# Even layer: the gating branch moved in front of the attention, and the queries and keys of heads 2 and 3 made inside it

## The chip, the cores and the metric

The kernel runs on one core of one Trainium2 chip (a trn2 part). The metric is the device time of one run in microseconds (us), the median of several runs. One further run was taken with the hardware profiler; all rows of the trace come from that run. The engines are PE (matrix products), DVE and POOL (elementwise work, reductions), ACT (activation functions and copies) and SP (which here issues transfers); they run side by side and wait for each other by semaphores.

## The reference, cut to what matters

The program is a two-layer block over 512 tokens and 256 context tokens, in float32, with a model width of 1024. The change lies in the mixer of layer 0, the even layer:

```python
u, v, q, k, vv = jnp.split(h @ w_in, [A_WIDTH, 2 * A_WIDTH, KV_START, KV_START + B_QK_WIDTH], axis=-1)
q = apply_rope(q.reshape(b, s_len, 2 * B_HEADS, HEAD_DIM), cos, sin)
k = apply_rope(k.reshape(b, s_len, 2 * B_HEADS, HEAD_DIM), cos, sin)
...
o = lax.map(lambda qb: diff_attn(qb, k_all, v_all, lam), q_blocks)
y = jnp.concatenate([chunk_mlp(u, v, w_s, b_s), diff_out(o, subln_g, lam_init)], axis=-1) @ w_out
```

There are two branches. The gating branch (`chunk_mlp`) takes `u` and `v`, four groups of 128 columns each: both go through an exact gelu, `v` is normalised over the 128 columns of a group, mixed along each chunk of 128 tokens by a matrix `w_s` of the group, and multiplied with `u`. The attention branch has four heads; each computes two softmaxes and subtracts `lam` times the second from the first (`diff_attn`). The context tokens go through the same steps with keys of the context alone. Both branches are laid side by side and projected with `w_out`.

## The kernel before, in words

Everything is kept with features on the partitions and tokens along the free axis: 512 token columns (TX) and 256 context columns (TC), 768 (TA) together. A float32 operand is split into a high and a low part of reduced precision, and each product is made of three matrix products (`mm3`, its lines L115, L116 and L117): high by high, high by low, low by high. The split of a weight block is a cast on ACT (L89) and a subtraction on POOL (L92); its load (L86) is issued on SP's queue. The buffers of loaded and split weights form a ring, so a load waits until an older buffer has been used.

The even layer runs in these stages, in the order in which PE meets them.

1. Queries and keys, in two halves. Half 0 makes those of heads 0 and 1, half 1 those of heads 2 and 3; each is 8 steps over the input features with 4 blocks of 128 columns, first for the tokens (512 wide) and then for the context (256 wide). Half 0 also normalises the inputs. Between the steps stand slabs of the modulation's weights (`ada_ahead` loads one, `ada_some` multiplies it, L370): work of another part of the layer that is laid here. The finished queries and keys go through `rope` (two DVE and two POOL operations each: shuffle L263, cosine L264, sine L265, sum L266).
2. The values V, 8 steps with 6 blocks of tokens, with one slab per step.
3. The attention, by head and, within a head, by pair of query blocks `qp`: 0 and 1 are tokens (scores against 768 keys), 2 is context (256 keys). One `softmax_diff` makes the scores (L553 and L554), their maximum (DVE, L555), the exponential (ACT, L557) and the difference (DVE, L563); `attend` then transposes it (PE, L575), splits it (ACT L131, DVE L132) and multiplies it with V. `stack` splits the queries and keys of the next head (ACT L272, L287, L288, DVE L276, L290). `norm` normalises a finished head.
4. Filling products. PE would stand still in the attention while a softmax runs. So `gated(i)`, one block of 128 columns of `u` (i = 0 to 3) or `v` (i = 4 to 7), 24 products of 512 and 24 of 256 columns, is given to the scheduler at a lower priority than the heads (`high_priority` lifts the heads above work written before them): it is taken where nothing of the heads is ready. In the kernel before, blocks 4 to 7 fill heads 0 and 1, and blocks 0 to 3 heads 2 and 3.
5. After head 1, the four gelus of `v` stand together on ACT (L643), and the exponentials of head 2 are held behind them (`issue_after(last.ins)`), so that ACT changes between the tables of gelu and exponential only there. Then `turn(g)` transposes a group of `v` on PE (L655), takes it back (ACT L656) and makes its statistics on DVE (L659 and L660); `mix(g)` normalises it (ACT L670, DVE L672), multiplies it with the mixing matrix (PE L673) and adds the bias (DVE L674). The mixes stand last, behind head 3.
6. `slab` loads the weights of the projection (`even_out`, 512 KB each), `cat` multiplies `u` and `v` (L717) and splits the eight inputs, and the projection (384 wide) follows.

The scheduler works out the order of each engine's instructions ahead of the run from priorities and from which operands are ready; on the chip every engine then goes through its own list strictly in order. SP's queue is such a list too.

## Time and profile before

| | |
|---|---|
| time, median of 3 runs | 1572.99 us (1571.8 to 1576.91) |
| time of the profiled run | 1574.88 us |
| its span in the trace | 1573.0 us |
| mean granted PE clock | 0.994 of full speed |
| busy: PE, DVE, ACT, POOL | 1514.1, 1073.0, 727.8, 826.1 us |

Of the span, the part that the change touches begins at 39.6 us (half 0 of the queries and keys) and ends at 333.7 us (first product of the projection). A row of the windows view gives a stretch of time, its length, the busy time of PE, of PE's weight loads, of DVE, ACT and POOL with their instruction counts, the granted PE clock (1.00 is full speed), the share of the transfer engines that was busy, and GB/s. A row of the timeline gives start, length, engine, line, operation and operands, and in brackets how long the engine had stood idle and what it waited for. A row of one line of code gives the shortest, the median and the longest duration in ns and the first and last start. Busy PE is not PE at full speed: where the clock is halved, each product simply takes longer.

### The profile page before, as it was taken

Reading aid. Unit: us, or ns where it says so; the run is one execution under the profiler, and the core shown is the slowest. Engines: PE = TensorE matmul, PEld = TensorE weight load, DVE = VectorE, ACT = ScalarE, POOL = GpSimd, SP = SyncE. Lnnn points to the kernel's source line nnn. Section 1 sums busy time; section 2 is a strip of 40 time slices with the busy share of each in tenths; the row PEclk is TensorE's granted clock in tenths of the full one; section 3 lists DMA queues with packets and bytes.
Section 4 is the critical chain, followed back from the end, with each engine's and each line's share of the span. In section 5 each row is a group of like instructions: output and inputs, shape, how many; then the busy total and the mean of one; then the engine's idle time right before and its main releaser. Section 6 shows DMA issues by size and latency. Waiting matters only on the chain.

```text
span 1573.0 us, 24994 instructions
## 1 busy us (share of the span) xinstructions
PE 1514.1 (96%) x9563; PEld 1352.0 (86%) x9563; DVE 1073.0 (68%) x1938; ACT 727.8 (46%) x1490; POOL 826.1 (53%) x558
## 2 busy tenths in 40 slices
PE   6999987999999999999999999999999999999998
PEld 4776876889999999999999988777869889999997
DVE  3720788765697787888786486765667966666665
ACT  2422677553553333333333354555645644444444
POOL 0464211050347777777776544531314399898982
PEclk9999999999999999999999999999999999999999
DMA  9835100033223333344542212200224133333301
GB/s 331 311 131 201 45 8 1 1 134 134 68 74 121 114 95 128 128 150 165 167 157 85 79 47 61 68 28 15 68 95 173 54 104 103 104 100 108 95 21 54
DMA packets 53416, 162.26 MB, mean 103 GB/s; under 512 B 6193, under 2 KB 8625, under 8 KB 45617
## 3 DMA queue, kind: packets, MB, share of 16 engines
q1 hardware_dynamic: 46240, 135.37, 25.7%
q10 hardware_dynamic: 7056, 25.30, 5.0%
q8 instruction: 75, 1.23, 0.3%
q14 instruction: 45, 0.36, 0.1%
HBM read 158.55 MB, written 2.10 MB: 102 GB/s over the span
## 4 chain that ended last, share of the span: by engine, by line
PE 85%; DVE 10%; ACT 3%; issue 1%; DMA 0%; DVEq 0%; SPq 0%; ACTq 0%
PE pw L115 12%; PE pw L116 12%; PE pw L117 11%; PE pb L116 8%; PE pb L117 8%; PE pb L115 8%; PE pf L115 4%; PE pf L116 4%; PE pf L117 4%; PE pb L1635 2%; PE pb L1624 2%; PE pf L370 2%; PE pw L1586 1%; PE pw L1594 1%; DVE t L49 1%
## 5 line engine op out<-in xcount | busy, mean ns | idle before, releaser
L116 PE MATMUL pw<-ax,w 128*128 128x384 f32 (+2 forms) x740 | 237.0, 321 | 3.5 <-DVE ax L49 2.2
L115 PE MATMUL pw<-ax,w 128*128 128x384 f32 (+2 forms) x740 | 235.9, 321 | 3.6 <-DVE q L49 1.9
L117 PE MATMUL pw<-ax,w 128*128 128x384 f32 (+2 forms) x740 | 236.4, 320 | 0.1
L785 DVE SCALAR_TENSOR_TENSOR xT<-pb,mod,xT 128x512 f32<-128x512 f32 (+3 forms) x204 | 143.2, 708 | 129.3 <-PE pb L117 128.8
L92 POOL TENSOR_TENSOR w<-raw,w 128x512 fp32r<-128x512 f32 (+1 forms) x76 | 115.4, 1526 | 219.0 <-ACT w L89 196.3
L49 POOL TENSOR_TENSOR w<-raw,w 128x512 fp32r<-128x512 f32 x122 | 185.0, 1531 | 48.8 <-ACT w L49 48.7
L49 POOL TENSOR_TENSOR w<-t,w 128x512 fp32r<-128x512 f32 x99 | 148.7, 1505 | 55.7 <-ACT w L49 55.7
L115 PE MATMUL pb<-hh,w 128*128 128x512 f32 x480 | 171.4, 357 | 1.2 <-DVE xT L785 1.2
L117 PE MATMUL pb<-hh,w 128*128 128x512 f32 x480 | 171.7, 358 | 0.4 <-DVE w L49 0.4
L116 PE MATMUL pb<-hh,w 128*128 128x512 f32 x480 | 171.3, 357 | 0.0
L115 PE MATMUL pw<-T,w 128*128 128x384 f32 (+1 forms) x508 | 156.6, 310 | 2.5 <-DVE hs L991 1.2
L116 PE MATMUL pw<-T,w 128*128 128x384 f32 (+1 forms) x508 | 157.0, 310 | 1.2 <-DVE T L132 1.2
L117 PE MATMUL pw<-T,w 128*128 128x384 f32 (+1 forms) x508 | 157.0, 310 | 0.0
L116 PEld LDWEIGHTS pw<-ax,w 128*128 128x128 f32 x740 | 140.8, 190 | 10.4 <-DVE ax L477 3.1
L115 PEld LDWEIGHTS pw<-ax,w 128*128 128x128 f32 x740 | 140.0, 190 | 10.6 <-DVE q L49 2.7
L115 PE MATMUL pf<-ax,w 128*128 128x256 f32 (+2 forms) x428 | 140.7, 329 | 3.9 <-ACT f L596 2.8
L117 PEld LDWEIGHTS pw<-ax,w 128*128 128x128 f32 x740 | 140.7, 190 | 3.3 <-DVE w L954 0.4
L116 PE MATMUL pf<-ax,w 128*128 128x256 f32 (+2 forms) x428 | 139.6, 326 | 0.0
L117 PE MATMUL pf<-ax,w 128*128 128x256 f32 (+2 forms) x428 | 139.5, 326 | 0.0
L49 POOL TENSOR_TENSOR hh<-hs,hh 128x768 fp32r<-128x768 f32 (+1 forms) x42 | 77.3, 1842 | 94.7 <-ACT hh L49 70.7
L49 POOL TENSOR_TENSOR w<-rawo,w 128x512 fp32r<-128x512 f32 x59 | 103.8, 1759 | 28.6 <-ACT w L49 28.6
L240 DVE SCALAR_TENSOR_TENSOR junk<-ar,cb 128x1024 bf16<-128x1024 f32 x64 | 105.7, 1651 | 0.0
(412 smaller groups left out, 3909.2 us busy)
## 6 DMA issues: line engine op xcount, KB each, us to landing
raw<-ffn_in SPq DMA_DIRECT2D x44, 1024.0 KB, 5.1
ar<-ada SPq DMA_DIRECT2D x24, 1024.0 KB, 6.8
ar<-ada ACTq DMA_DIRECT2D x48, 512.0 KB, 3.6
rawo<-ffn_out SPq DMA_DIRECT2D x88, 256.0 KB, 3.0
raw<-odd_out SPq DMA_DIRECT2D x28, 256.0 KB, 2.7
raw<-qk SPq DMA_DIRECT2D x16, 256.0 KB, 7.9
raw<-uv SPq DMA_DIRECT2D x16, 256.0 KB, 2.7
raw<-even_out SPq DMA_DIRECT2D x8, 512.0 KB, 3.9
```

The source lines that it names most:

```text
L49: self.tail[key] = fn(*args, **kw)
L92: eng.tensor_tensor(lo, raw, hi.bitcast(F32), ALU.subtract)
L115: mm(out, s[0], m[0], start=start, stop=False, **kw)
L116: mm(out, s[0], m[1], start=False, stop=False, **kw)
L117: return mm(out, s[1], m[0], start=False, stop=stop, **kw)
L240: return self.nc.vector.scalar_tensor_tensor(junk, t, 1.0, self.cb[who], ALU.mult, ALU.mult, accum_out=self.acc[who][:, col:col + 1])
L370: nc.tensor.matmul(ps[32 * q:32 * q + 32, :w], cst[:, k, :], t[:, w * q:w * q + w], start=k == 0, stop=k == KT - 1, skip_group_check=True)
L785: ins = self.nc.vector.scalar_tensor_tensor(h, ps[:, r], self.modcol(l, j, m, who), h, ALU.mult, ALU.add)
L1586: nc.tensor.matmul(ps[:, st:en], Q, K[g][p][:, b0 * P:b1 * P], start=p == 0, stop=p == 1, skip_group_check=True)
L1594: last = nc.tensor.matmul(ps[:, en:en + TC], Q, K[g][p][:, TX:], start=p == 0 and not edge, stop=p == 1, skip_group_check=True)
L1624: last = nc.tensor.transpose(pt[:, x * P:(x + 1) * P], es[2 * (x % 2) + x // 2][:, kb * P:(kb + 1) * P], self.ident)
L1635: nc.tensor.matmul(po[64 * h:64 * h + 64, :], V[vb][:, 64 * g:64 * g + 64], t[:, h * TC:h * TC + TC], start=kb == 0, stop=kb == nb - 1, sk ...
```

## The change

In the front part only heads 0 and 1 get their queries and keys. Half 1 is cut out, and with it the place of six slabs, which now stand in the V stage, two at every second step. The weights of heads 2 and 3 are laid out anew on the host (`qk1`) as four blocks of 128 columns, like those of `gated`.

Behind V comes the gating branch of `v`: `gated(4)` to `gated(7)` one after the other, each followed by its gelu, with `turn` one block behind; then `lam`, the reciprocal roots of the statistics and the four `mix`. Their PSUM banks come from `bank` in place of `fill`. Then come the heads. They are filled by `block(0)` to `block(3)` (queries and keys of heads 2 and 3, with their rope) in heads 0 and 1, and by `gated(0)` to `gated(3)` in heads 2 and 3. The gelus of `u` and the product with `v` stay where they were, behind the last exponential. Buffers move with it: the rope tables stay to the end of the attention, its shuffle buffer has one copy in place of two, the pool `f3` has four slots in place of eight and the four `v` have a tag of their own.

```diff
+        self.ropep = tc.alloc_tile_pool(name="rope0", bufs=1, side="left", reuse_waits="tile")
+        self.sh_bufs = 1
+        self.ropep.tile([P, 512], F32, name=self.uid("sh"), tag="sh", bufs=1)
+        tabs = [self.ropep.tile([P, TX], F32, name=n, tag=n, bufs=1) for n in ("cos", "sin")]
...
-        def f3(tag="f3", bufs=8):
+        def f3(tag="f3", bufs=4):
             return R1.tile([P, TA], F32, name=self.uid(tag), tag=tag, bufs=bufs)
...
-        tabs = []
...
-        for half, heads in enumerate(((0, 1), (2, 3))):
-            w2 = [self.wide(), self.wide()]
-            accx = [w[:, h * 512:(h + 1) * 512] for w in w2 for h in range(2)]
-            W = []
...
-                elif k % 2:
-                    ada_ahead(1)
-                    ada_some()
...
+        w2 = [self.wide(), self.wide()]
+        accx = [w[:, h * 512:(h + 1) * 512] for w in w2 for h in range(2)]
+        keys = (0, 1, 4, 5)
+        W = []
+        for k in range(KT):
+            t = self.adap.tile([P, 2, 512], F32R, name=self.uid("wq"), tag="wq", bufs=2) if k in (2, 5) else None
+            with tc.issue_after(self.last_slab.ins):
+                W.append(self.blocks(a["qk"][k], 512, t=t))
+                if k > 3:
+                    with tc.issue_after(self.last_w.ins):
+                        ada_ahead(1)
+                if k == 7:
+                    for t, n in zip(tabs, ("cos", "sin")):
+                        nc.sync.dma_start(t, a[n])
...
+            if k % 2:
+                ada_some()
+                ada_ahead(1)
+        for n in range(4):
+            evacuate(accc[n], keys[n], slice(TX, TA))
+        for n in (0, 4, 1, 5):
+            self.rope(qk[n][:, :TX], qk[n][:, :TX], tabs)
...
                 self.mm3(acc[tb], [t[:, c] for t in AX_[k]], W, k == 0, k == KT - 1)
-            ada_ahead(1)
-            ada_some()
+            for _ in range(1 + k % 2):
+                ada_some()
+                ada_ahead(1)
         for ps in acc:
             h = Rv.tile([P, 512], F32R, name=f"vhi{len(vhi)}")
             l = Rv.tile([P, 512], F32R, name=f"vlo{len(vhi)}")
@@ -525,13 +521,12 @@
             ada_ahead(1)
             ada_some()
         with tc.issue_after(self.last_w.ins):
-            sguT = self.load(Rv, a["sguT"], [P, 512], "sguT")
+            sgu = self.sumsq()
+            sguT = sgu[:, :512]
+            nc.sync.dma_start(sguT, a["sguT"])
             sgub = self.load(Rv, a["sgub"].partition_broadcast(P), [P, 512], "sgub")
-        here = tc.cur_priority
-        self.ropep.release()
         self.adap.release()
 
-        self.lam()
         self.subg = self.load(self.p0, a["subln"], [P, 1], "subg")
...
         def gated(i, after=None):
 
             W = self.blocks(a["uv"][i])
-            u = f3()
+            u = f3() if i < 4 else f3("rv")
             for off, T, A in ((0, TX, axx), (TX, TC, axc)):
-                ps = self.fill()[:, :T]
+                ps = (self.fill if off or i < 4 else self.bank)()[:, :T]
                 self.dense(ps, W, A, after, 0 if off else 2)
                 nc.scalar.copy(u[:, off:off + T], ps)
             raw[i] = u
...
-        def gelu(i, after):
-            with tc.issue_after(after.ins):
+        def gelu(i, after=None):
+            with tc.issue_after(after.ins) if after else ExitStack():
                 return nc.scalar.activation(raw[i], raw[i], AF.Gelu)
 
         halves = ((0, 4), (4, 2))
-        stats = Rv.tile([P, 24, 6], F32, name="stats")
+        stats = sgu[:, 512:656].rearrange("p (t v) -> p t v", v=6)
...
-        with tc.high_priority(offset=tc.cur_priority - here):
-            QK = {0: stack(0)}
-        for t in range(2):
-            head(t)
+        def block(n):
+
+            key = (2, 6, 3, 7)[n]
+            W = self.blocks(a["qk1"][n])
+            qk[key] = f3()
+            for c, A in ((slice(0, TX), axx), (slice(TX, TA), axc)):
+                ps = self.fill()[:, :c.stop - c.start]
+                self.dense(ps, W, A)
+                evacuate(ps, key, c)
+            self.rope(qk[key][:, :TX], qk[key][:, :TX], tabs)
+
+        QK = {0: stack(0)}
+        for g in range(4):
+            gated(4 + g)
+            last = gelu(4 + g)
+            if g:
+                turn(g - 1)
+        turn(3)
+        with tc.issue_after(last.ins):
+            self.lam()
+        rs = self.rstd_small(mv[:, :, 1], 24, 1.0, "sf")
+        nb = self.small(24, "sf", 3)
+        nc.vector.scalar_tensor_tensor(nb, mv[:, :, 0], -1.0, rs, ALU.mult, ALU.mult)
+        for g in range(4):
+            mix(g, rs)
         here = tc.cur_priority
-        for i in (4, 5, 6, 7):
-            gated(i)
-        for i in (4, 5, 6, 7):
-            last = gelu(i, self.last_exp)
-        with tc.high_priority(offset=tc.cur_priority - here), tc.issue_after(last.ins):
-            head(2)
-            head(3)
-        after = self.last_sum
-        for g in range(4):
-            turn(g)
-            gated(g, after if g == 3 else None)
+        for t, jobs in enumerate(((block, 0, 1), (block, 2, 3), (gated, 0, 1), (gated, 2))):
+            for i in jobs[1:]:
+                jobs[0](i, *([self.last_exp] if t == 3 else []))
+            with tc.high_priority(offset=tc.cur_priority - here), tc.issue_after(last.ins):
+                head(t)
+        gated(3, self.last_sum)
         Ra.release()
+        self.ropep.release()
+        self.sh_bufs = 2
         self.close_ring()
         self.ada_open(2)
         self.open_ring(1024, 3, 8)
...
         slab(0)
         slab(1)
-        rs = self.rstd_small(mv[:, :, 1], 24, 1.0, "sf")
-        nb = self.small(24, "sf", 3)
-        nc.vector.scalar_tensor_tensor(nb, mv[:, :, 0], -1.0, rs, ALU.mult, ALU.mult)
-        for g in range(4):
-            mix(g, rs)
         cat = {}
         for k in order:
             if k < 4:
...
+    qk = ew[:, 1024:2048].reshape(D, 2, 2, 2 * P)
+    r["qk"] = c(qk[:, :, 0].reshape(KT, P, 512))
     r["v0"] = c(ew[:, 2048:2560])
...
+    r["qk1"] = cols(c(qk[:, :, 1].reshape(D, 2, 2, P).transpose(0, 2, 1, 3).reshape(D, 512)))
     r["uv"] = cols(ew[:, 0:1024])
```

The scheduler's order shows what comes of it. The rows below are PE's around the first scores of head 0; `ax` with `w` is a filling product or one of `gated`, `kh`, `kl` with `qa`, `qb` are scores, `ident` is a transposition. In the kernel before, the first scores stand behind the 512 wide half of the first `gated` alone:

```order
L116 MATMUL pf_1914<-ax_326,w_1910 128x512
L117 MATMUL pf_1914<-ax_325,w_1910 128x512
L553 MATMUL pw_1344<-kh_1328,qa_1322 128x512
L554 MATMUL pw_1344<-kh_1328,qa_1322 128x256
L553 MATMUL pw_1344<-kl_1329,qa_1322 128x512
...
L554 MATMUL pw_1352<-kl_1335,qb_1323 128x256
L115 MATMUL pf_1940<-ax_311,w_1905 128x256
L116 MATMUL pf_1940<-ax_312,w_1905 128x256
```

In the changed kernel they stand behind all four `gated` of `v` and the transpositions of its group 2 (`rv_1221`), and the block that follows them is one of queries and keys:

```order
L116 MATMUL pf_1334<-ax_329,w_1304 128x256
L117 MATMUL pf_1334<-ax_328,w_1304 128x256
L650 MATMUL pb_1361<-ident_103,rv_1221 128x128 x4
L650 MATMUL pb_1375<-ident_103,rv_1221 128x128 x2
L548 MATMUL pw_1635<-kh_1049,qa_1043 128x512
L549 MATMUL pw_1635<-kh_1049,qa_1043 128x256
...
L549 MATMUL pw_1643<-kl_1056,qb_1044 128x256
L115 MATMUL pf_1506<-ax_314,w_1497 128x512
...
L116 MATMUL pf_1506<-ax_325,w_1502 128x512
L650 MATMUL pb_1383<-ident_103,rv_1307 128x128 x4
L117 MATMUL pf_1506<-ax_324,w_1502 128x512
```

What moved is three and a half blocks of `gated` and three of the four turns to a place ahead of the scores; the last turn and the mixes lie within head 0.

The next rows are ACT's between the last exponentials of head 3 (`e`) and the first cast of the projection's weights (`w_3133<-raw_3134` before, `w_3217<-raw_3218` in the changed kernel). Before, the normalisation of the mixes (L670, twelve in all) and the copies of the turns stand there:

```order
L557 ACTIVATE e_2715,sa_2704<-pw_2711,sa_2703 128x256
L643 ACT_TABLE_LOAD
L643 ACTIVATE f_555_2810<-f_555_2810 128x768
L643 ACTIVATE f_564_2895<-f_564_2895 128x768
L131 CAST ath_2637<-pb_2632 128x512
...
L656 COPY f_375_2102<-pf_3047 128x256
L587 COPY o_2459<-pb_2722 128x256
L612 ACTIVATE sq_2739<-o_2459 128x768
L670 ACTIVATE f_354_1913<-f_354_1913,sf_3156,sf_3144 128x128 x3
L670 ACTIVATE f_361_1976<-f_361_1976,sf_3156,sf_3144 128x128 x3
...
L643 ACTIVATE f_582_3065<-f_582_3065 128x768
L89 CAST w_3133<-raw_3134 128x1024
```

In the changed kernel they are gone, and all three gelus of `u` stand ahead of the last splits of the difference (`ath`), since the blocks of `u` are done earlier:

```order
L552 ACTIVATE e_3075,sa_3064<-pw_3071,sa_3063 128x256
L638 ACT_TABLE_LOAD
L638 ACTIVATE f_405_2340<-f_405_2340 128x768
L638 ACTIVATE f_412_2403<-f_412_2403 128x768
L638 ACTIVATE f_503_2766<-f_503_2766 128x768
L131 CAST ath_3012<-pb_3007 128x512
L131 CAST ath_3027<-pb_3022 128x512
...
L131 CAST ath_3088<-pb_3083 128x512
L582 COPY o_2819<-pb_3082 128x256
...
L131 CAST ax_3240<-f_405_2340 128x768
L638 ACTIVATE f_597_3148<-f_597_3148 128x768
L131 CAST ax_3246<-f_412_2403 128x768
L89 CAST w_3217<-raw_3218 128x1024
```

The third place is PE's list behind the last scores of head 3 (`pw` with `kh` and `kl`, 256 wide). Before, filling products (`pf_2981`) stand right behind them, and the transpositions of the difference come between these:

```order
L165 MATMUL pb_2561<-ones,sq_2457 128x128 x2
L554 MATMUL pw_2711<-kh_2390,qb_2379 128x256
L554 MATMUL pw_2711<-kl_2391,qb_2379 128x256
L115 MATMUL pf_2981<-ax_311,w_2972 128x512
L116 MATMUL pf_2981<-ax_312,w_2972 128x512
...
L117 MATMUL pf_2981<-ax_317,w_2972 128x512
L575 MATMUL pb_2632<-ident_100,e_2593 128x128
L115 MATMUL pf_2981<-ax_319,w_2977 128x512
...
L117 MATMUL pf_2981<-ax_325,w_2977 128x512
L115 MATMUL pb_2631<-ath_2637,vhi_1274 128x256
```

In the changed kernel the scores are followed by transpositions and products with V (`ath`, `vhi`) alone, and the filling products `pf_3149` come again behind the head's last sum of squares (L165), since `gated(3, self.last_sum)` holds all but their first six back:

```order
L549 MATMUL pw_3071<-kh_2687,qb_2676 128x256
L549 MATMUL pw_3071<-kl_2688,qb_2676 128x256
L115 MATMUL pb_2991<-ath_2997,vhi_1007 128x256
L570 MATMUL pb_3007<-ident_103,e_2953 128x128
...
L117 MATMUL pb_2991<-ath_3027,vlo_1028 128x256
L195 MATMUL pb_3038<-q_2937,ones 128x512
L195 MATMUL pb_3041<-q_2942,ones 128x256
L570 MATMUL pb_3083<-ident_103,e_3050 128x128
...
L117 MATMUL pb_3082<-ath_3088,vlo_1028 128x256
L165 MATMUL pb_3102<-ones,sq_3099 128x128 x4
L165 MATMUL pb_3108<-ones,sq_3099 128x128 x2
L115 MATMUL pf_3149<-ax_318,w_3140 128x512
```

What moved is the filling: of 72 and 72 filling products (512 and 256 wide) behind the first scores of head 3, the changed kernel has 24 and 48 left.

More of the change, by code (lines that the diff above doesn't have):

```diff
@@ L447, in ctx_load, with evacuate @@
                 hc.extend(t[:, n, :] for n in range(4))
-        tabs = []
-        def evacuate(ps, n, c, heads):
-            h = heads[n % 2]
-            key = h if n < 2 else 4 + h
-            if key not in qk:
-                qk[key] = f3()
-            nc.scalar.mul(qk[key][:, c], ps, 0.125 if n < 2 else 1.0)
+        for key in (0, 4, 1, 5):
+            qk[key] = f3()
+        def evacuate(ps, key, c):
+            nc.scalar.mul(qk[key][:, c], ps, 0.125 if key < 4 else 1.0)
         with tc.issue_after(self.last_slab.ins):
@@ new lines, in even @@
+        for n in range(4):
+            evacuate(accx[n], keys[n], slice(0, TX))
+        bk = [self.bank() for _ in range(2)]
+        accc = [b[:, h * TC:(h + 1) * TC] for b in bk for h in range(2)]
+        for k in range(KT):
+            for n in range(4):
+                self.mm3(accc[n], W[k][n], axc[k], k == 0 and n % 2 == 0, k == KT - 1)
+            if k % 2:
+                ada_some()
+                ada_ahead(1)
+        for n in range(4):
+            evacuate(accc[n], keys[n], slice(TX, TA))
@@ L652, in turn @@
             for off, n in halves:
-                ps = self.fill()
+                ps = self.bank()
                 for i in range(n):
@@ L665, in mix @@
             for off, n in halves:
-                pw = self.fill()
+                pw = self.bank()
                 for i in range(n):
```

50 lines of the change are left out of this document (12 added, 38 removed).

## The prediction

> **What bounds the kernel now.** I read the page first, for the engines' shares and for the chain that ends last:
>
> ```profile
> PE 1514.1 (96%) x9563; PEld 1352.0 (86%) x9563; DVE 1073.0 (68%) x1938; ACT 727.8 (46%) x1490; POOL 826.1 (53%) x558
> PE 85%; DVE 10%; ACT 3%; issue 1%; DMA 0%; DVEq 0%; SPq 0%; ACTq 0%
> ```
>
> PE bounds the whole, so a moved product wins nothing by itself; only PE's waits can be won or lost. The windows view, cut at the stages and at the heads' first scores, shows where these lie (columns: stretch, length, then busy PE, weight loads, DVE, ACT, POOL; clock; share of the transfer engines; GB/s):
>
> ```profile
> 39.60:81.80 42.20, 40.50 (x231) 30.99 (x232) 28.98 (x51) 20.29 (x39) 21.18 (x15) 1.00 0.79 290
> 81.80:121.80 40.00, 40.00 (x242) 30.54 (x243) 10.04 (x20) 7.82 (x16) 26.85 (x20) 1.00 0.45 156
> 121.80:163.40 41.60, 41.60 (x206) 28.13 (x206) 7.21 (x10) 13.35 (x21) 14.52 (x12) 1.00 0.46 167
> 163.40:169.00 5.60, 5.59 (x25) 4.30 (x23) 5.56 (x10) 3.81 (x8) 1.80 (x2) 1.00 0.23 67
> 169.00:200.60 31.60, 29.61 (x184) 26.09 (x184) 21.83 (x40) 18.86 (x40) 6.66 (x4) 1.00 0.12 39
> 200.60:214.60 14.00, 12.66 (x77) 11.28 (x78) 12.73 (x23) 9.44 (x20) 3.37 (x2) 1.00 0.07 20
> 214.60:250.30 35.70, 27.61 (x160) 22.96 (x158) 28.43 (x70) 26.36 (x50) 4.37 (x3) 0.86 0.00 0
> 250.30:271.60 21.30, 19.44 (x130) 17.48 (x130) 17.09 (x44) 15.46 (x34) 3.40 (x3) 1.00 0.00 1
> 271.60:294.70 23.10, 21.97 (x140) 19.55 (x141) 20.43 (x53) 12.84 (x29) 1.20 (x1) 1.00 0.00 1
> 294.70:333.70 39.00, 35.06 (x220) 29.20 (x219) 27.70 (x115) 24.72 (x50) 5.83 (x3) 1.00 0.19 68
> 333.70:352.00 18.30, 18.30 (x116) 18.30 (x115) 12.69 (x11) 8.31 (x9) 15.59 (x7) 1.00 0.45 144
> ```
>
> PE never waits in half 1 (81.8 to 121.8), in V or in the projection behind 333.7. It loses 18.3 us between the first score at 169.0 and the projection at 333.7, and the worst stretch is 214.6 to 250.3: 8.1 us idle, and more lost to a clock of 0.86. ACT's timeline shows what stands there, the gelus of `v` between two table loads:
>
> ```profile
> 234.41 0.20 ACT L557 ACTIVATION_READ_ACCUMULATOR e<-pw,sa 128x1 f32 x1
> 234.63 1.28 ACT L643 ACT_TABLE_LOAD   x1
> 235.92 3.04 ACT L643 ACTIVATE f<-f 128x768 f32<-128x768 f32 x4
> 238.87 0.83 ACT L272 ACTIVATE qa<-f 64x768 fp32r<-64x768 f32 x1
> ...
> 241.90 1.28 ACT L557 ACT_TABLE_LOAD   x1
> ```
>
> From 234.4 to 243.2 ACT makes no exponential. In PE's timeline the products with V stand 0.12 us apart ahead of the hole and 0.21 behind it, half the rate:
>
> ```profile
> 237.24 0.28 PE L115 MATMUL pb<-ath,vhi 128*128 128x256 f32 x1
> 237.36 0.28 PE L116 MATMUL pb<-atl,vhi 128*128 128x256 f32 x1
> ...
> 241.94 0.47 PE L115 MATMUL pb<-ath,vhi 128*128 128x256 f32 x1 [1.54 <-ACT ath L131]
> 244.24 0.79 PE L553 MATMUL pw<-kh,qa 128*128 128x512 f32 x1 [1.84 <-ACT e L557]
> ...
> 248.25 0.41 PE L115 MATMUL pb<-ath,vhi 128*128 128x256 f32 x1
> 248.46 0.41 PE L116 MATMUL pb<-atl,vhi 128*128 128x256 f32 x1
> ```
>
> **Step 1: the front.** The price of a product is the distance of two starts. For 256 columns it is the 0.12 above; for 512 columns it is 0.23, since 163.4 to 169.0 holds the 24 wide products of one block in 5.6 us. A block of 24 and 24 products thus costs 5.5 + 2.9 = 8.4 us. Half 1 is 96 and 96 of them, 4 × 8.4 = 33.5 us; the other 6.5 us of its 40.0 are the six slabs, which go to V at the same price. What comes in ahead of the first score is three blocks of `gated` and the 256 wide half of the fourth, 25.2 + 2.9 = 28.1, and 18 transpositions of the turns with their switches, an estimate of 2.2 from the 0.1 us of a 128 wide product (below). First score: 169.0 − 33.5 + 28.1 + 2.2 = 165.8. The gelus and statistics there lie beside 33 us of products; nothing of PE reads them before the turn one block later.
>
> **Step 2: the attention, by stretch.** The filling products that the order puts into each stretch (512 and 256 wide) are, before: 48 and 48; 21 and 24; 3 and 24; 24 and 24; 24 and 24; 48 and 48. After: 72 and 72; 24 and 24; 48 and 24; 24 and 24; 6 and 24; 18 and 24. What else moves is priced from these rows:
>
> ```profile
> 339.68 1.05 PE L673 MATMUL pf<-sguT,f 128*128 128x128 f32 x8
> L659 DVE BATCH_NORM_STATS2 stats<-pf x24: 274/282/300, 244.8 to 316.2; 128x6 f32<-128x128 f32 x24
> L660 DVE BATCH_NORM_AGGREGATE mv<-stats x24: 146/167/186, 247.2 to 316.5; 128x2 f32<-128x6 f32 x24
> L672 DVE TENSOR_SCALAR f<-f,mv,sf x12: 341/344/347, 319.8 to 322.8; 128x128 f32<-128x128 f32 x12
> L674 DVE TENSOR_TENSOR f<-pf,sgub x8: 414/552/692, 330.8 to 354.9; 128x512 f32<-128x512 f32 x4, 128x256 f32<-128x256 f32 x4
> L263 DVE STREAM_SHUFFLE sh<-f x8: 739/742/761, 77.0 to 118.0; 128x512 f32<-128x512 f32 x8
> L264 DVE TENSOR_TENSOR f<-f,cos x8: 693/976/993, 77.7 to 118.8; 128x512 f32<-128x512 f32 x8
> L265 POOL TENSOR_TENSOR sh<-sh,sin x18: 1277/1296/1810, 77.8 to 1046.3; 128x512 f32<-128x512 f32 x18
> L290 DVE TENSOR_TENSOR kl<-f,kh x12: 942/954/1994, 163.0 to 270.2; 64x768 fp32r<-64x768 f32 x12
> ```
>
> *Head 0* (31.6 before). PE: 29.6 + one more block 8.4 + the mixes 4.9 (48 records, 8 in 1.05 with the last one's tail, so about 0.1 each) + a turn 0.6 = 43.5. DVE: 21.8 + 12 statistics with their aggregates (12 × 0.45 = 5.4) + 11 small operations of the reciprocal root (an estimate of 0.17 each from L660, 1.9) + 12 × 0.34 (L672, 4.1) + 8 × 0.55 (L674, 4.4) + three ropes at 0.74 + 0.98 (5.2) + five splits of 0.95 for the next head, which the order puts earlier (4.8) = 47.6. DVE goes past PE here; I take 48.0.
>
> *Head 1's first pair* (14.0): PE 12.7 + 0.7 = 13.4; I take 13.5. *Head 1's rest and head 2's first pair* (35.7): at full clock PE's own products are about 22 (27.6 less 5 for the slow clock), with 45 wide products more (10.4) and six transpositions fewer about 32; DVE 28.4 + two ropes 3.4 − six statistics 2.7 = 29.1. The hole is filled and its two table loads are gone from it; I take 34.0, 2 us of waits left. *Head 2's rest* (21.3): a turn leaves; 20.5. *Head 3, two pairs* (23.1): 18 wide products leave PE (22.0 − 4.1 = 17.9), DVE's 20.4 bounds it; 21.3.
>
> *The end, from head 3's context to the projection* (39.0): PE loses 30 wide and 24 narrow products (9.8), the first 20 records of the mixes (2.0) and eight transpositions: about 22. But now it is this place that has no filling, and the table load of gelu (1.28) and three gelus of 0.76 (the four of 3.04 above) stand ahead of the last splits. The nearest row is the unfilled stretch of before, which lost 8.1: 22 + 8 = 30. From below it would lose 3.9, as now (26); from above 8.1 and the 5 of the slow clock (35).
>
> Sum: 165.8 + 48.0 + 13.5 + 34.0 + 20.5 + 21.3 + 30.0 = 333.1, against 333.7.
>
> **Step 3: the projection.** From 333.7 on 28 records of the mixes stand between its products on a PE that is always busy; they go: −2.8. In all −3.4 on the span of 1573.0: 1569.6. The profiled run took 1574.88, 1.9 above its span, and the median is 1572.99; −3.4 on the median gives 1569.6 too. **I forecast 1569.6 us**, 0.2% faster. What a measurement of this kernel can tell from no change is about 0.3%, 4.7 us.
>
> [...] DVE's split behind `stack` and POOL's subtraction of a weight block ran at the same time once:
>
> ```profile
> 162.95 2.73 DVE L290 TENSOR_TENSOR kl<-f,kh 64x768 fp32r<-64x768 f32 x2
> 161.94 1.96 POOL L92 TENSOR_TENSOR w<-raw,w 128x512 fp32r<-128x512 f32 x1 [6.21 <-ACT w L89]
> ```
>
> Two splits took 2.73, not 1.9; the first ended 1.0 late, and POOL ended at 163.90, 0.95 after it began. [...]
>
> **Rivals.** *First, the hole goes and nothing takes its place.* Head 0 then costs PE's 43.5, as the mixes' DVE work is urgent for nobody, and the end loses only 3.9: −4.5 − 4.1, so 1561. For it: DVE has slack in all later stretches, and the twelve normalisations, 4.73 in the row below, leave ACT's end. Against it: every engine takes its list in order, and head 0's splits stand behind the statistics.
>
> ```profile
> 319.94 4.73 ACT L670 ACTIVATE f<-f,sf,sf 128x128 f32<-128x128 f32 x12 [2.00 <-DVE sf L710]
> ```
>
> *Second, slower: DVE in head 0, held up by POOL.* The four ropes bring eight POOL operations of 1.3 us into heads 0 and 1, six of them into head 0. If each holds up one two-input operation of DVE for up to its length (the pair above: 1.0), that is 6 to 8 us where DVE already is the bound; and `lam` now makes DVE wait, in order, for a small transfer issued behind the last gelu, with statistics and maxima of head 0 queued behind it; 2 to 3 us, an estimate from the 2.7 that a block of `uv` takes to land (the slowest weights, those of `qk`, take 7.9):
>
> ```profile
> raw<-qk SPq DMA_DIRECT2D x16, 256.0 KB, 7.9
> raw<-uv SPq DMA_DIRECT2D x16, 256.0 KB, 2.7
> ```
>
> Head 0 at 58: 1580. From 51.4 us of head 0 on the gain is gone, and from 56 on the kernel is slower by more than 0.3%.
>
> *Third, the projection starts late.* In SP's queue the inputs' reload now stands ahead of the last three slabs of the projection, and the first cast on ACT behind the fourth gelu: a slab's cast (1.0 below) and a wait of a few us for a slab, +5: 1575. Against it: the slabs needed first are issued at the same event as before, the end of head 3.
>
> ```profile
> 330.37 1.97 ACT L89 CAST w<-raw 128x1024 fp32r<-128x1024 f32 x2
> ```
>
> *Fourth, the front doesn't shrink.* Half 0 already moved 290 GB/s at a share of 0.79; one slab more ahead of V, and V's waits for slabs, would take back 3 to 4 us: 1573. Against it: V moved 167 GB/s at 0.46.
>
> **How the numbers follow.** Forecast 0.54 (own range 1563 to 1575, from 43.5 to 51 in head 0 and 26 to 35 at the end, which partly cancel), first rival 0.16, second 0.16, third 0.07, fourth 0.07. The range from 1558 to 1581 takes in both sides. Faster by over 0.3% (below 1568.3): a little under half of the forecast's cases, 0.25, and the first rival: 0.40. Slower (above 1577.7): the second rival, and a tenth for mishaps in the third, fourth and the forecast's upper end: 0.25. Within: 0.35.
>
> **What would show it.** First score near 165.8 (later: fourth rival). Head 0 near 48 with DVE busy throughout (43.5: first; past 51: second). No half clock in 214 to 250 of before's place, one at the end of head 3. The projection's first product at 333, and then no mixing records between its products. The forecast is wrong if head 0 or the end misses by more than 5 us.

## The result and the profile after

The changed kernel takes 1581.64 us (median of 11 runs, 1577.05 to 1585.7), the kernel before, in the same series, 1575.57 (11 runs, 1571.8 to 1577.17). The ratio is 1.0038, interval 1.0026 to 1.0051: **slower by 0.4%**, where 0.2% faster was forecast. The profiled run is one of the lower times: 1577.26, with a span of 1575.4, 2.4 above before's. The profiled runs of e4 and e9 below fell in a disturbed state of the chip (clock 0.655 and 0.751), so none of their rows is read and their times come from the other runs.

Page of after, busy time by engine:

```profile
PE 1514.1 (96%) x9563; PEld 1354.2 (86%) x9563; DVE 1079.9 (69%) x1938; ACT 726.3 (46%) x1489; POOL 826.5 (52%) x558
```

PE is busy for the same 1514.1 us in both kernels, so the spans differ by PE's waits; time that a slow clock costs lies hidden within the busy time. Windows view of after, cut at the same events as before's (its columns too): first scores of the heads, the projection's first product, then 40 us of the projection.

```profile
0.00:164.30 164.30, 149.71 (x921) 108.75 (x922) 61.08 (x135) 56.73 (x106) 51.99 (x43) 1.00 0.64 233
164.30:212.60 48.30, 45.31 (x291) 40.10 (x290) 43.28 (x113) 33.13 (x70) 14.51 (x11) 1.00 0.12 36
212.60:225.40 12.80, 12.80 (x80) 11.49 (x80) 12.63 (x23) 6.70 (x16) 6.08 (x5) 1.00 0.08 22
225.40:260.40 35.00, 31.92 (x197) 27.64 (x195) 31.20 (x67) 22.04 (x48) 9.43 (x6) 1.00 0.00 0
260.40:280.70 20.30, 18.81 (x131) 17.19 (x129) 15.97 (x34) 12.20 (x27) 0.61 (x1) 1.00 0.00 1
280.70:299.90 19.20, 18.38 (x121) 16.03 (x121) 18.50 (x48) 12.84 (x29) 1.22 (x1) 1.00 0.00 1
299.90:334.80 34.90, 23.61 (x134) 19.26 (x134) 22.40 (x69) 17.57 (x33) 3.60 (x3) 0.89 0.22 76
334.80:353.00 18.20, 18.20 (x90) 18.20 (x91) 13.04 (x5) 6.13 (x7) 15.29 (x5) 0.84 0.46 161
353.00:375.00 22.00, 20.90 (x114) 19.14 (x113) 2.89 (x6) 8.03 (x9) 7.19 (x3) 1.00 0.58 225
```

Up to 299.9 every stretch came within 1.0 us of its forecast or better; the old hole (225 to 260) runs at clock 1.00. The loss begins in the stretch to 334.8 (34.9 long, 11.3 of it idle, clock 0.89) and goes on in the projection (clock 0.84, then 1.1 us idle), where PE was full at clock 1.00 before. PE's waits in that stretch of after, from the waits view (total, times, longest):

```profile
PE pw L115 <- ACT w L89: 3.6, 1, 3.6
PE pb L115 <- ACT ath L131: 3.5, 3, 2.5
PE pb L116 <- DVE atl L132: 2.8, 4, 1.4
PE pb L165 <- ACT sq L607: 1.3, 1, 1.3
```

The longest is the projection's first product, for the cast of its first weight slab. ACT's timeline of after says why that cast is late:

```profile
306.51 1.28 ACT L638 ACT_TABLE_LOAD   x1
307.80 2.31 ACT L638 ACTIVATE f<-f 128x768 f32<-128x768 f32 x3
...
327.12 0.59 ACT L591 COPY f<-pf 128x512 f32<-128x512 f32 x1 [5.85 <-PE pf L117]
328.58 2.30 ACT L131 CAST ax<-o 128x768 fp32r<-128x768 f32 x3 [0.88 <-PE pf L116]
331.21 0.37 ACT L591 COPY f<-pf 128x256 f32<-128x256 f32 x1 [0.32 <-PE pf L117]
331.48 0.83 ACT L131 CAST ax<-f 128x768 fp32r<-128x768 f32 x1
332.21 0.84 ACT L638 ACTIVATE f<-f 128x768 f32<-128x768 f32 x1
332.96 0.82 ACT L131 CAST ax<-f 128x768 fp32r<-128x768 f32 x1
333.68 1.04 ACT L89 CAST w<-raw 128x1024 fp32r<-128x1024 f32 x1
```

ACT idles 5.85 us for the last 512 wide filling product (`gated(3)`), then works through that block's two copies, five input splits and the fourth gelu before it casts slab 0. And the later casts wait for their slabs. From the transfers of `even_out` and the casts' waits, after first, then before:

```profile
DMA to landing us min/median/max: 3.5/4.9/11.9
  DMA raw<-even_out: 24.5, 5
```

```profile
DMA to landing us min/median/max: 3.4/3.9/7.1
  DMA raw<-even_out: 4.7, 2
```

Five casts wait 24.5 us in all for slabs that land up to 11.9 after issue; before, two waited 4.7. The table load and the three gelus at 306.51 stand ahead of the splits of `ath`, and PE's 2.5 us wait for `ath` ends behind them.

Last, the clock. In the traces of before and after, all changes of the granted clock lie whole multiples of 3.413 us apart, on one grid in each trace; these windows of after are cut on it:

```profile
306.30:309.70 3.40, 1.44 (x11) 1.06 (x9) 2.09 (x9) 3.37 (x6) 0.00 (x0) 1.00 0.00 0
309.70:316.60 6.90, 4.60 (x14) 3.47 (x15) 4.93 (x15) 1.75 (x4) 0.00 (x0) 0.51 0.00 0
316.60:320.00 3.40, 2.36 (x13) 1.53 (x11) 1.83 (x3) 0.59 (x1) 0.00 (x0) 1.00 0.00 0
330.20:333.60 3.40, 0.97 (x9) 0.77 (x7) 1.46 (x2) 3.08 (x5) 3.31 (x2) 1.00 0.00 0
333.60:340.50 6.90, 5.73 (x18) 5.73 (x19) 6.90 (x4) 5.22 (x7) 5.98 (x3) 0.51 0.21 69
```

The grid windows with 1.44 and 0.97 us of work were followed by half clock (0.51), the one with 2.36 was not. The second half-clock stretch lies in the projection, on a PE that is full.

### The profile page after: what moved, and what is told of

The parts are those of the page before. It is cut to its first block, busy times and chain, and to the rows that moved or that the text cites. A ratio compares the mean times of both kernels' runs of the same rounds, so it can differ in the third digit from the quotient of the medians.

```text
span 1575.4 us, 25009 instructions
## 1 busy us (share of the span) xinstructions
PE 1514.1 (96%) x9563; PEld 1354.2 (86%) x9563; DVE 1079.9 (69%) x1938; ACT 726.3 (46%) x1489; POOL 826.5 (52%) x558
## 4 chain that ended last, share of the span: by engine, by line
PE 79%; DVE 14%; ACT 2%; issue 2%; DMA 2%; POOL 0%; SPq 0%; DVEq 0%; ACTq 0%; POOLq 0%
PE pw L115 10%; PE pw L116 10%; PE pw L117 10%; PE pb L116 8%; PE pb L117 8%; PE pb L115 8%; PE pf L115 3%; PE pf L116 3%; PE pf L117 3%; PE pb L1643 2%; PE pb L1632 2%; PE pf L373 2%; PE pw L1594 1%; DMA raw<-even_out 1%; PE pw L1602 1%
## 5 line engine op out<-in xcount | busy, mean ns | idle before, releaser
L115 PE MATMUL pw<-ax,w 128*128 128x384 f32 (+2 forms) x716 | 227.4, 320 | 7.8 <-ACT w L89 4.2
L116 PE MATMUL pw<-ax,w 128*128 128x384 f32 (+2 forms) x716 | 227.8, 318 | 3.5 <-DVE ax L49 2.2
L117 PE MATMUL pw<-ax,w 128*128 128x384 f32 (+2 forms) x716 | 227.4, 319 | 0.6 <-POOL w L92 0.3
L115 PE MATMUL pf<-ax,w 128*128 128x256 f32 (+2 forms) x460 | 150.0, 326 | 1.1 <-DVE qf L264 1.1
L117 PE MATMUL pf<-ax,w 128*128 128x256 f32 (+2 forms) x460 | 148.5, 323 | 0.0
L116 PE MATMUL pf<-ax,w 128*128 128x256 f32 (+2 forms) x460 | 148.2, 322 | 0.0
L115 PEld LDWEIGHTS pw<-ax,w 128*128 128x128 f32 x716 | 136.0, 191 | 13.2 <-ACT w L89 5.0
L116 PEld LDWEIGHTS pw<-ax,w 128*128 128x128 f32 x716 | 136.7, 191 | 8.6 <-DVE ax L49 2.7
L117 PEld LDWEIGHTS pw<-ax,w 128*128 128x128 f32 x716 | 136.6, 191 | 3.7 <-POOL w L92 1.5
```

Of the source, the lines that this page charges most:

```text
L115: mm(out, s[0], m[0], start=start, stop=False, **kw)
L116: mm(out, s[0], m[1], start=False, stop=False, **kw)
L117: return mm(out, s[1], m[0], start=False, stop=stop, **kw)
```

## The experiments

Theory S (supply): the loss is the projection's supply, in two parts, the slabs queued behind the reloads on SP (2.6 us behind the start) and slab 0's cast late on ACT (3.6 ahead of it), with the half clock behind them. Rival F (filling): the end merely lacks products, as the old hole did, and filling it is what counts. Rival T: the table loads of gelu made the old hole, and now make the end's. Rival K: the clock halves whatever is mended, and only moves. The expectations, word for word as on record, use letters of their own: theory A is mostly S, theory B is K or F, each explained where it stands; theory C, in e10 and e11, is that the filling of the end is worth its 4 us and that the two fillings before e10 lost them to POOL, so that e10 comes out 2 to 4 us below the kernel before. Ratios are to the kernel before, on the same chip, and edits are against the changed kernel unless another is named. "Product for product" sets the start of each matrix product against that of the same product in another trace.

**e1: the changed kernel once more**, unaltered.

> The changed kernel once more, unaltered, beside the kernel before on one chip. Its eleven times fall into two groups, five near 1577.2 us and six from 1580.9 to 1585.7, whose granted clock is 0.993 and 0.990; the profiled run is of the first group. Theory A (supply: the last three slabs of the projection stand behind the reloads in SP's queue, and the first slab's cast stands late in ACT's list) expects both groups again and, where a profile of the upper group is met, longer waits of PE for the slabs between 340 and 375 us. Theory B (clock: PE's waits in the unfilled end of head 3 and ahead of the projection let the clock fall to half, for more or fewer of the clock's windows) expects the two groups to differ in the clock between 300 and 350 us alone, with the same waits for slabs. Median 1580 by both.

Measured: 1582.7, ratio 1.0039 (1.0023 to 1.0055). The slowdown stands; profile and half-clock windows are those of after to 0.3 us.

**e2: the last three slabs ahead of the reloads.**

```diff
+        self.even_w = self.last_w
+        with tc.issue_after(self.even_w.ins):
+            self.hxs, hcs = [[self.load(pool, a[x][r, :].rearrange("(k p) t -> p k t", p=P), [P, nh, T], f"{x}{r.start}")
...
+            with tc.issue_after(self.even_w.ins):
+                self.ffn_open(0, cat)
```

> One alteration of the changed kernel: the reloads of the inputs and of the first weights behind them are held back in SP's queue until all eight slabs of the projection have been issued, as in the kernel before. Theory A expects the casts' waits of 10.0, 5.7 and 4.2 us for slabs to go, and with them the 2.6 us that the products lose between 358 and 375 us: span 1572.8, and the upper group of times to go or to come down by as much. Theory B expects 2.6 us less in the profile too, but the two groups to stay some 6 us apart, since the clock ahead of 350 us is untouched.

Measured: 1580.2, ratio 1.0026 (1.0017 to 1.0035). The same rows as above, of e2:

```profile
DMA to landing us min/median/max: 3.4/3.5/5.3
  DMA raw<-even_out: 10.6, 5
```

The slabs land in 3.5 and the casts' waits fall from 24.5 to 10.6. Product for product, e2 makes up 2.6 us on after between 357 and 393, as expected. But its span is 1576.2, not shorter, since its profile has two half-clock windows ahead, at 42.9 and 251.1 (+1.3 and +1.6), in code that is still that of after. At the second place, e2, then after:

```profile
247.70:251.10 3.40, 1.33 (x8) 0.94 (x7) 3.40 (x4) 1.55 (x4) 3.32 (x3) 1.00 0.00 0
251.10:254.50 3.40, 3.40 (x13) 3.04 (x13) 3.40 (x10) 1.94 (x4) 0.34 (x1) 0.50 0.00 0
```

```profile
244.90:248.30 3.40, 2.86 (x20) 2.40 (x19) 3.34 (x5) 3.27 (x10) 3.08 (x2) 1.00 0.00 0
248.30:251.70 3.40, 1.90 (x13) 1.78 (x14) 3.40 (x9) 0.24 (x1) 2.05 (x2) 1.00 0.00 0
```

The same gap falls into one grid window in e2 (1.33 us of work, then half clock) and is shared by two in after (2.86 and 1.90, no half clock). Between these two profiles, what differed was where the grid stood when the gap came.

**e3: slabs 0 and 1 cast ahead of all input splits.**

```diff
 slab(1)
-cat = {}
+first_casts, cat = self.last_cast, {}
...
-    self.split(*cat[k], src, nc.gpsimd if k in (5, 6) else nc.vector)
+    with tc.issue_after(first_casts.ins):
+        self.split(*cat[k], src, nc.gpsimd if k in (5, 6) else nc.vector)
```

> One alteration: on ACT the casts of the first two slabs stand ahead of the casts of the projection's inputs (in the changed kernel the first slab, issued at 319.9, is cast at 333.7 behind six other operations, and PE waits 3.6 us for it). SP's order moves with it: only the last slab stands behind the reloads of xT. Theory A expects the first product of the projection 2 to 3 us earlier (332) and most of the 2.6 us behind it to go as well: span 1570 to 1571. Theory B expects the start to be earlier by the same and, as the wait of 3.6 us is what halves the clock at 334.8 to 345 (0.72), another 2 to 3 us from the clock: span 1568 and one group of times.

Measured: 1583.0, ratio 1.004 (1.0025 to 1.0054). A miss of the edit, and a lesson: the first product waits about as long as in after (3.95 against 3.60), now for its other operand.

```profile
337.92 1.01 PE L115 MATMUL pw<-ax,w 128*128 128x384 f32 x2 [3.95 <-ACT ax L131]
```

**e4: the last filling block released by the last score instead of the last sum.**

```diff
-gated(3, self.last_sum)
+gated(3, self.last_score)
```

> One alteration: the last block of filling products (gated(3)) is held back only to head 3's last scores, no longer to its last sum of squares, so that it fills the softmax of head 3's context. Theory B (the unfilled end costs the time, by its waits of 6.6 us between 299.9 and 320 and the clock of 0.89 that follows) expects the first product of the projection at 329, 5 to 6 us earlier, with the clock at 1.00 up to 320: span 1569. Theory A expects PE to wait for the first slab instead, since it is issued only at the end of head 3 and needs some 8 us to land, be cast and be split: the projection's start at 331 to 333 and a span of 1572 to 1574.

Measured: 1581.9, ratio 1.0036 (1.0023 to 1.0049): nothing gained. e8, which has this edit too, shows where such a gain can go; that e4 lost it in the same way is likely, not shown.

**e5: slab 0's cast ahead of all splits but the first, and of the last block's second copy** (`late`, the context half of `gated(3)`).

```diff
 slab(0)
+cast0 = self.last_cast
 slab(1)
+with tc.issue_after(cast0.ins):
+    nc.scalar.copy(*late)
...
-    self.split(*cat[k], src, nc.gpsimd if k in (5, 6) else nc.vector)
+    with tc.issue_after(cast0.ins) if k != order[0] else ExitStack():
+        self.split(*cat[k], src, nc.gpsimd if k in (5, 6) else nc.vector)
```

> One alteration of the changed kernel: on ACT only the cast of the first slab moves ahead of the copy of the last filling product's context half and of five of the six casts of the projection's inputs; the first input's cast stays ahead of it. (With all input casts behind two slab casts, the start came 0.4 us later and the products behind it 4 us later.) Theory A (supply: ACT's list feeds the projection too late) expects the 3.6 us of waiting ahead of the projection to go: first product at 331.5, with the clock at full rate there, since nothing idles from 322 on: 3 to 6 us less in the profile, span 1570 to 1572. Theory B (the clock, whatever starts it) expects the start to come 3 us earlier, but the group of slower times to remain, since the unfilled end of head 3 is the same.

Measured: 1582.1, ratio 1.0031 (1.0018 to 1.0044). The 3.6 us wait is gone, but the stretch still takes 34.6. Windows of e5, on the grid:

```profile
319.40:322.80 3.40, 1.73 (x11) 1.09 (x9) 1.17 (x2) 1.17 (x3) 0.00 (x0) 1.00 0.00 0
322.80:329.60 6.80, 6.12 (x20) 5.37 (x21) 2.94 (x17) 0.63 (x1) 0.00 (x0) 0.50 0.91 313
```

Its waits up to here are those of after, but on another phase of the grid 1.73 us of work fall into one window, and two windows of half clock follow, in which the fillers run. Product for product, these two cost 2.9 us of the 3.8 that the earlier start wins. In the projection PE then waits for late slabs.

**e6: both edits, e2 and e5; e11: the same kernel on the chip of e10.**

```diff
+with tc.issue_after(cast0.ins):
+    nc.scalar.copy(*late)
...
+        with tc.issue_after(self.even_w.ins):
```

> Both supplies mended: the eight slabs ahead of the reloads in SP's queue, and the first slab's cast early on ACT. Theory A: 2.6 + 3 to 6 us less than the changed kernel, span 1567 to 1570 in a profile with the same clock windows ahead of it, median 5 to 8 us below the changed kernel's 1582.7 on the same chip, thus level with the kernel before or below it. Theory B: the median comes down by the 5.6 us of waits, but the times still spread over 5 us or more, as the half clock of head 3's end comes and goes.

> The run with both supplies mended once more, on the same chip as the one with POOL held back, so that the two can be compared: level with the kernel before, within 0.15%, and 2 to 4 us above the other by theory C, equal to it by theory B.

Measured: e6 1576.9, ratio 0.9991 (0.9979 to 1.0004), and e11 1575.94, ratio 0.9985 (0.9974 to 0.9997). Beside e5, on the same chip, e6 is 5.2 us quicker, while e2 alone won 2.5 on e1 and e5 alone 1.3 (by its ratio against e1's): the parts don't add. e5's profile shows one reason, the windows of half clock that took most of what its start had won. Product for product, e6 gains 3.8 us on after at the projection's start and 3.2 more behind it; two half-clock windows further ahead, as in e2, cost it 2.9. The end takes 30.9 in e6 and, in this row, 31.4 in e11:

```profile
300.60:332.00 31.40, 23.74 (x134) 19.43 (x135) 19.92 (x67) 13.42 (x26) 0.52 (x1) 0.89 0.24 85
```

Theory S holds: with both parts of the supply mended, and nothing else, the changed kernel is level with the one before or 0.15% quicker. Rival K has a share too: the end of e6 and e11 still runs at clock 0.89, and e6's twelve times still spread over 8.3 us.

**e7: the kernel before with its four gelus of `v` made copies**, so that no table is loaded in its hole. It leaves out those gelus.

```diff
-return nc.scalar.activation(raw[i], raw[i], AF.Gelu)
+return nc.scalar.activation(raw[i], raw[i], AF.Identity if i > 3 else AF.Gelu)
```

> The price of the hole in the kernel before: its four gelus of v are replaced by a copy function that needs no table (the computation leaves out these four gelus), so that two table loads go (2.6 us) and nothing else moves in that place. If the tables make the hole (what the prediction gave as its cause), PE's waits between 234 and 250 us shrink by 2.6 us or more and the half clock of 231.9 to 248.9 goes: span 1573 - 5 = 1568. If the lack of filling products makes it, the waits and the half clock stay but for 1 us: span 1571 to 1573.

Measured: 1575.1, ratio 0.9989 (0.9978 to 1.0000), with a span of 1571.8. Head 2's first pair, with the hole, takes 13.9 instead of 16.8, in these rows of before and e7:

```profile
233.60:250.40 16.80, 11.64 (x51) 9.23 (x51) 13.73 (x40) 13.15 (x22) 1.80 (x1) 0.75 0.00 0
```

```profile
234.10:248.00 13.90, 9.83 (x52) 8.13 (x52) 12.94 (x38) 10.36 (x20) 1.80 (x1) 0.88 0.00 0
```

4.1 of the 13.9 stay idle with no table loaded, against 5.2 of the 16.8. Tables were some 3 us of the old hole, with the clock that they cost: T explains a part. That F is the rest is supported by after's filled stretch (225 to 260), which idles 3.1 of 35.0 us at full clock, but no run filled the hole alone. Nor did any run take the table load and the gelus out of the end.

**e8: e2 and e4 together.**

```diff
+with tc.issue_after(self.even_w.ins):
...
-gated(3, self.last_sum)
+gated(3, self.last_score)
```

> The last filling block within head 3's context (as in the run with the filled end) and the eight slabs ahead of the reloads. Theory A: the first slab is issued at the end of head 3's last product with V, at about 320, and PE then has nothing to do until it is cast at about 326: the products with V end no later, but PE waits 6 to 8 us there, and the start comes at 328 to 330; in all 5 to 7 us less than the changed kernel, unless the clock falls in that wait. Theory B: the wait of 6 to 8 us in one piece halves the clock there for one or two windows (1.7 to 3.4 us), where the end of head 3 keeps it: 2 to 4 us less than the changed kernel.

Measured: 1583.1, ratio 1.003 (1.0018 to 1.0042). The filling works: the first product of the projection comes at 326.45, 8.3 earlier than in after. Then PE stands still again. PE, DVE and POOL timelines of e8:

```profile
340.42 2.93 PE L195 MATMUL pb<-q,ones 128*128 128x512 f32 x4 [7.10 <-DVE q L185]
```

```profile
326.07 0.17 DVE L147 SCALAR_TENSOR_TENSOR sm<-sm,sm 128x6 f32<-128x6 f32 x1
...
329.59 2.33 DVE L148 SCALAR_TENSOR_TENSOR sm<-sm,sm 128x6 f32<-128x6 f32 x1
331.95 2.30 DVE L146 TENSOR_TENSOR sm<-sm 128x6 f32<-128x6 f32 x1
334.29 2.27 DVE L147 SCALAR_TENSOR_TENSOR sm<-sm,sm 128x6 f32<-128x6 f32 x1
336.59 2.26 DVE L148 SCALAR_TENSOR_TENSOR sm<-sm,sm 128x6 f32<-128x6 f32 x1
```

```profile
326.47 12.35 POOL L92 TENSOR_TENSOR w<-raw,w 128x1024 fp32r<-128x1024 f32 x5 [3.59 <-ACT w L89]
```

The norm of head 3 is a chain of small DVE operations (the reciprocal root) that PE's `q` products wait for. They take 0.17 us alone and 2.3 while POOL subtracts weight slabs, 2.47 each: four of them lose 8.5 us. This is the prediction's second rival, at another place.

**e9: e6, with the token half of the last block released by the last score and the context half by the last sum; e10: the same, and slab 0's cast held behind that block's last copy**, so that POOL starts after the root chain (the last two lines are e10's alone).

```diff
-gated(3, self.last_sum)
+late = gated(3, self.last_score, hold=self.last_sum)
...
+with tc.issue_after(late.ins):
+    slab(0)
```

> Both supplies mended, and of the last filling block the token half (18 products of 512 columns, 4.1 us) stands right behind head 3's last scores, its context half (2.9 us) still behind the head's last sum of squares, so that the root of the last normalisation on DVE is over before POOL subtracts the first slabs. Theory A (what is left is the unfilled end: 8 us of waits between the last scores and the end of head 3) expects the end of the products with V at the same time, 3 to 4 us less behind it, the first product of the projection 3 us earlier than with the supplies alone, no half clock between 305 and 320, and a median 3 to 5 us below the kernel before. Theory B (the clock, whatever starts it): PE then waits behind the context half for the first slab, 2 to 3 us in one piece, and the half clock moves there: level with the supplies alone, within 1.5 us of the kernel before.

> As the run with the half fill, but the first slab's cast on ACT stands behind the copy of the filling product's context half, so that POOL's subtraction of that slab begins after DVE has made the last normalisation's root (11 small operations) and its six diagonals. In the two fillings before, those operations stood between POOL's and took up to 2.4 us each in place of 0.17, and PE waited 7.1 and 12.1 us for them in the midst of the projection's first products. [...] Theory B (the clock): the wait for the slab, now about 2 us, brings a half clock there, and the time is that of the supplies alone.

Measured: e9 1582.8, ratio 1.003 (1.0018 to 1.0041), a miss; **e10 1571.97 (1570.3 to 1574.7), ratio 0.9969 (0.9954 to 0.9984), quicker than both kernels.** Windows, DVE, POOL and PE timelines of e10:

```profile
300.10:328.40 28.30, 22.88 (x133) 19.26 (x133) 19.48 (x66) 14.60 (x29) 0.00 (x0) 0.94 0.26 93
```

```profile
325.36 0.17 DVE L148 SCALAR_TENSOR_TENSOR sm<-sm,sm 128x6 f32<-128x6 f32 x1
```

```profile
328.51 2.42 POOL L92 TENSOR_TENSOR w<-raw,w 128x1024 fp32r<-128x1024 f32 x1 [46.39 <-DVE f L728]
```

```profile
327.10 1.56 PE L195 MATMUL pb<-q,ones 128*128 128x512 f32 x4 [0.94 <-DVE q L185]
```

POOL starts at 328.51, the roots are done and take 0.17 each, `q` is waited for 0.94 instead of 7.10, and the end takes 28.3. So filling gains too, but only with POOL out of the way: beside e11, on the same chip, 4.0 us of the median (the two intervals still overlap). e9 differs from e10 in that place alone, but its rows are not read; that POOL was its loss too is taken from e8's rows and e10's gain. In the two profiles e10's end is 3.1 shorter than e11's. Product for product, 2.5 of it are left at 400 and 1.3 at 970; a half-clock window at 1217.9, which e11 does not have, takes 1.5, so that the two spans are alike (1570.2 and 1569.7). The 4 us stand on the medians; the traces show 1.3 to 2.5 of them.

## Why the prediction was wrong

**Step 1, the front: right.** 164.3 against 165.8 (0.5 of the difference lies ahead of 39.6, where nothing was changed); the fourth rival fell.

**Step 2 up to head 3: right, and with the front 3.2 us better than forecast.** Head 0 took 48.3 against 48.0. That it came so near is in part luck: DVE was not busy throughout, as forecast, but for 43.3, not 47.6, and PE for 45.3, not 43.5; three waits of PE make up the rest. POOL did hold up DVE there. Timelines of DVE and POOL in after:

```profile
178.62 1.25 DVE L559 SCALAR_TENSOR_TENSOR sx<-sa 128x1 f32<-128x1 f32 x1
182.33 0.15 DVE L559 SCALAR_TENSOR_TENSOR sx<-sa 128x1 f32<-128x1 f32 x1
```

```profile
177.78 2.07 POOL L266 TENSOR_TENSOR f<-f,sh 128x512 f32<-128x512 f32 x1 [0.69 <-DVE mv L655]
```

Two such tiny operations took 1.25 and 1.26 us instead of 0.15 and 0.21, a difference (L558) 1.79 instead of 1.02, and six splits 1.11 on average instead of 0.95: some 4 us in all, about half of the second rival's 6 to 8, on an engine that stood idle for 5.0 of the 48.3. The other stretches came to 12.8, 35.0, 20.3 and 19.2, against 13.5, 34.0, 20.5 and 21.3. The old hole did go.

**Step 2, the end: failed, 34.9 against 30.0.** The middle itself was sound: 22 of work and 8 lost for want of filling, against 21.3 (23.6, less 2.3 for half clock on 4.6 us of work) and 7.7 idle. What was left out stands on top: 3.6 for slab 0's cast and the 2.3 of the slow clock. The prediction had the second in its upper end of 35, and the first in its third rival, as separate cases, although its list of signs expected a half clock at the end of head 3. Both stand in the place that the filling and the mixes left, and they came together; e5, which lost the first and kept a half clock, shows that they are two things.

**Step 3, the projection: failed, +1.3 against −2.8.** The mixing records did leave (90 products in 18.2 us at clock 0.84, where 116 took 18.3 at full clock). In their place stand half clock on 5.7 us of work (+2.9) and the late slabs (+2.6, as e2 bears out). That sums to +2.7; the other −1.4 stays open (product for product, 0.6 of it lies between 1215 and 1245, far from the change). The third rival's argument against itself, that the slabs needed first are issued at the same event, was true and beside the point: that event, the end of head 3, now comes at 319.9 instead of 316.6, and the cast and the reloads stand behind it in the lists of ACT and SP.

**In all:** −3.2 up to 299.9, +4.9 in the end, +4.1 behind it (each measured less forecast) make +5.8, the span of 1575.4 against the 1569.6 of the sum. The third rival was the right one, with 0.07 for it: its two delays, forecast at +5, measured 3.6 and 2.6. That its 1575 meets the span is luck, though: half clock came on top with 5.2, and 5.6 came back elsewhere (3.2 up to 299.9, 1.0 in the middle of the end, and the open 1.4). Its price belonged in the sum, since both delays stood in the orders of SP and ACT that the prediction had read.

**The medians lie 6 us apart, the profiled spans 2.4.** The times of after fall in two groups, four runs from 1577.05 to 1577.36 (mean clock 0.993 to 0.994) and seven from 1580.9 to 1585.7 (0.989 to 0.992); the expectation of e1 counts five and six. e2's and e3's profiles show how that can come about: the same code, on another phase of the grid, pays two more windows (2.9 us). Which windows the upper group pays wasn't traced, so the rest of the 6 us is put down to the clock by inference. Whether fewer gaps narrow the spread is not shown: e10's seven times lie within 4.4 us, but so do, at 4.5, e2's twelve. And 2.6 of the 12.0 us between the forecast and 1581.64 are no matter of the change: the forecast stood on a median of 1572.99 over three runs of the kernel before, whose eleven runs have 1575.57.

## What to carry to other kernels

Work that fills another engine's waits has a second job where it stands last: it covers the start of the next stage. Before moving it forward, go to the place it leaves and list, on each queue, what the next stage's first operands stand behind; a wait there costs its length and, in these traces, often a half clock behind it. Where a stage's start is pulled forward, look at which engines hold up the chain that still runs: e8 lost to POOL what its filling had won, and e10 kept a part by starting POOL a few microseconds later. And where times come in groups, compare medians of many runs and read the clock's windows before explaining a difference of 2 us between two traces.

## What the runs showed of the hardware

**In before and after, the clock followed how much PE had done in the grid window before; none of the windows ahead of a half clock was idle.** In these two traces (from 25 us on), 10 full-clock windows of 3.413 us held 0.58 to 1.50 us of PE's work, and all 10 were followed by half clock; 884 held 1.67 us or more, and none was. No single amount parts them in all runs: e5's window with 1.73 us was followed by half clock. The two half-clock windows of e2 cost 1.3 and 1.6 us. Ahead of after's two halvings in the end stood 1.44 and 0.97 us of products. In the kernel before, the first halving, at 231.9, came behind a window with 0.85 us of work and a wait of 2.51 us, longer than the 1.54 and 1.84 that the prediction's rows show; that wait lies ahead of the gelus' table load at 234.63, and is shorter than a window. PE's timeline of before:

```profile
231.60 0.39 PE L554 MATMUL pw<-kh,qb 128*128 128x256 f32 x1 [2.51 <-ACT e L557]
```

**Short DVE operations took many times their length beside POOL operations**: 0.17 us became 2.3 beside POOL operations of 2.47 (e8), and 0.15 became 1.25 beside one of 2.07 (after). In e8 four in a row lost 8.5 us, where a single split there lost 1.5 (2.50 instead of 0.96): the chain of four lost more than the one longer operation.
